# A second MLP product in seven block products for the latent tokens, its gate row formed on TensorE and its operand sums on GpSimd

## The chip, the cores and the metric

The kernel runs as one program on one core of a Trainium2 chip. The metric is device time of one execution in microseconds. TensorE (PE in the profile; PEld is its weight load) does the matrix products, VectorE (DVE) and ScalarE (ACT) the elementwise work, GpSimd (POOL) very little before the change, and SyncE (SP) issues nearly all DMAs.

## The reference, cut to what matters

One layer of a hybrid backbone over 640 tokens: 128 context tokens and 512 latent tokens, width 1024. The four mixers before the MLP are not touched by the change. What is touched is the end:

```python
shift1, scale1, gate1, shift2, scale2, gate2 = jnp.split(mod[:, None, :], 6, axis=-1)   # mod = silu(c) @ ada_w + ada_b
h2 = rmsnorm(x, norm2_g) * (1 + scale2) + shift2
ff = jnp.square(jax.nn.relu(h2 @ mlp_w1)) @ mlp_w2      # 640x1024 @ 1024x4096, then 640x4096 @ 4096x1024
x = x + gate2 * ff                                      # then one final rmsnorm
```

All of it is float32. Context rows use the gate of c_ctx, latent rows that of c.

## The kernel before, in words

**Precision.** Each float32 product is three passes in the type fp32r: an operand is split into a high part (a copy on ACT) and a low part (source minus high part, on DVE), and high x high, high x low and low x high are summed in PSUM. `split(hi, lo, src)` is this pair of instructions.

**The first MLP product** runs in 16 units of 256 columns of W1. A unit computes a 2x2 block product in seven block products (X11, X12, S2, S1, S3, S4, X22 of the weights with operands of the activations), each of 12 matmuls of 320 columns. The weight operands come from four raw blocks in WQ: sums of blocks on DVE (`sums`), then `split` into a ring XH/XL of 8 slots, made ahead of PE by up to 8 products. A unit holds a pair of PSUM banks A_ and B_. ACT copies a bank out and DVE adds the other (`rb<-ps,rb`, 128x320); then the bank is written on. So three DVE adds of a unit stand between products: the first half of r0 before S1 writes B_, the second half of r1 before X22 writes A_, the second half of r0 before the bank is used again. After them ACT applies Relu and Square to r0 and r1 (640 columns), and two splits store them as AH/AL (tiles olo).

**The second MLP product** is done per group of two units (8 groups, 512 rows of W2): four row blocks of W2 are loaded to w2raw and split into VH/VL (tiles vh, vl; 128x1024); for each of five token tiles, 4 x 3 passes x 2 halves = 24 matmuls of 512 columns, 120 in a group; DVE adds the result to ACC (tiles h), ten 128x512 adds in a group (ACT copies in the first group).

**gate2** is formed on DVE: the rows silu(c) are broadcast, and in groups 1 to 4 eight slices of ada_w are multiplied and summed along rows (`scalar_tensor_tensor` with an accumulator, 32 of 128x512). The finished row is broadcast after group 4.

**Order.** From the output projection on, all instructions are recorded and a planner (class Plan) emits them: PE keeps the recorded order; each other engine takes, among what its cost table holds to be ready, the instruction that is due first. Each engine then runs its list in that order. The table prices a GpSimd operation at 0.3 us plus n/450 us and a DVE one at 0.15 us plus n/960 us, each engine by itself. All these instructions have line 248 in the profile; they are told apart by tiles.

Of the kernel before, what the change touches and what calls it, by code (L numbers as in the profile page):

```python
# [7 lines left out]
F32 = mybir.dt.float32  # L8
# [400 lines left out]
def hybrid_step_kernel(ctx: ExitStack, tc: tile.TileContext, A: dict, O: dict):  # L409
# [860 lines left out]
    yhi["T2"], yhi["T3"], ylo["T2"], ylo["T3"] = pieces  # L1270
    AH, AL = oT["lo"][0:4], oT["lo"][4:8]
    PT = [tiles(psN, 2, [512], f"ps{i}_") for i in range(4)]

# [133 lines left out]

    NU, EARLY = 16, 4
    names = ("X11", "X12", "S2", "S1", "S3", "S4", "X22")
# [52 lines left out]

    rrot = [0]

    def next_r():
        rrot[0] = (rrot[0] + 1) % 3
        return RB[rrot[0]]

    def relu2(i, r):
        act.activation(r, r, AF.Relu)  # L1470
        act.activation(r, r, AF.Square)
        split(AH[i], AL[i], r)

    def unit(u, i):
        if u >= EARLY:
            first_products(u)
        A_, B_ = PT[ub[u]]
        a, b = A_[:, :HT], B_[:, :HT]
        r0, r1 = next_r(), next_r()
        act.activation(r0[:, :HT], a, AF.Copy)  # L1480
        dve.tensor_tensor(r0[:, :HT], b, r0[:, :HT], OP.add)
        product(u, "S2", "T2", A_, False)
        act.activation(r0[:, HT:], a, AF.Copy)
        product(u, "S1", "T1", B_, True)
        act.activation(r1[:, HT:], b, AF.Copy)
        product(u, "S3", "T3", A_, False)
        dve.tensor_tensor(r1[:, HT:], a, r1[:, HT:], OP.add)
        product(u, "S4", "Y22", B_, False)
        dve.tensor_tensor(r0[:, HT:], b, r0[:, HT:], OP.add)
        relu2(i, r0)  # L1490
        product(u, "X22", "T4", A_, False)
        act.activation(r1[:, :HT], a, AF.Copy)
        relu2(i + 1, r1)
        held.remove(ub[u])


    NG = 8
    half2 = lp.tile([128, 2, 8], F32, name="half2")

    def load_w2(g):  # L1500
        for i in range(4):
            raw = WRAW2[i % 2]
            nc.sync.dma_start(raw, A["w2"][2 * g + i // 2][:, D * (i % 2):D * (i % 2) + D])
            split(VH[i], VL[i], raw)

    def mm2(t, i, ps, halves=(0, 1)):
        ts_ = slice(128 * t, 128 * t + 128)
        for pi, (lh, rh) in enumerate(((AH, VH), (AH, VL), (AL, VH))):
            for n in halves:
                pe.matmul(ps[n], lh[i][:, ts_], rh[i][:, HALVES[n]], start=(i == 0 and pi == 0),  # L1510
                          stop=(i == 3 and pi == 2))

    def silu_rows():
        broadcast(flat(GATE), A["ccr"])
        jk = BIG[1][:, :512]
        for i in range(4):
            c = flat(GATE)[:, 512 * i:512 * i + 512]
            act.activation(jk, c, AF.Sigmoid)
            dve.tensor_tensor(c, c, jk, OP.mult)

    def gate2_part(i):
        wt, jk = BIG[0], BIG[1][:, :512]
        nc.sync.dma_start(wt, A["ada_g"][i])
        for cnd in range(2):
            for n in range(2):
                c = slice(512 * n, 512 * n + 512)
                dve.scalar_tensor_tensor(jk, wt[:, c], 1.0, GATE[:, cnd, c], op0=OP.mult, op1=OP.mult,
                                         accum_out=half2[:, n, cnd:cnd + 1])
            m = mod["gt2"][:, i, cnd:cnd + 1]
            dve.tensor_tensor(m, half2[:, 0, cnd:cnd + 1], half2[:, 1, cnd:cnd + 1], OP.add)  # L1530
            dve.tensor_tensor(m, m, P("adab", 40 + i), OP.add)

    fg = BIG[0]

    def finish_gate2():
        d = gate_rows("gt2", nc.sync)
        broadcast(flat(GATE), d)
        broadcast(fg, A["fg"])

    XA = []  # L1540

    def start_last():
        for t in range(NCH):
            XA.append(rp.tile([128, 4 * HT], F32, name=f"xa{t}", tag=("yh0", "yh1", "yl0", "yl1", "yh2")[t])[:, :D])
            nc.sync.dma_start(XA[t], x1d[t])
        for t in range(NCH):
            for n, c in enumerate(HALVES):
                a = ACC[n][:, t, :]
                dve.tensor_tensor(a, a, GATE[:, 0 if t == 0 else 1, c], OP.mult)
                dve.tensor_tensor(XA[t][:, c], XA[t][:, c], a, OP.add)  # L1550

    def last_tile(t, ps):
        x, y = XA[t], WRAW2[t % 2]
        for n, c in enumerate(HALVES):
            dve.tensor_tensor(y[:, c], ps[n], GATE[:, 0 if t == 0 else 1, c], OP.mult)
        dve.tensor_tensor(x, x, y, OP.add)
# [9 lines left out]
    def very_last(pairs):  # L1566
# [61 lines left out]
    first_products(2)  # L1628
    first_products(3)
    for g in range(NG):  # L1630
        last = g == NG - 1
        load_w2(g)
        for i in range(2):
            unit(2 * g + i, 2 * i)
        if last:
            start_last()
        pair = [PT[bank_pair()] for _ in range(2)]
# [4 lines left out]
        for t in range(NCH):  # L1642
            if last and t == NCH - 1:
# [6 lines left out]
            if last:  # L1650
                last_tile(t, ps)
                continue
            for n in range(2):
                a = ACC[n][:, t, :]
                if g == 0:
                    act.activation(a, ps[n], AF.Copy)
                else:
                    dve.tensor_tensor(a, ps[n], a, OP.add)
        if g == 0:
            silu_rows()  # L1660
        if 0 < g < 5:
            for i in range(2):
                gate2_part(2 * g - 2 + i)
        if g == 4:
            finish_gate2()
    with tc.manual_schedule():
# [3 lines left out]
def _arrays(inp):  # L1670
# [41 lines left out]
    for g, nm in enumerate(("rg_w_r", "rg_w_i")):  # L1712
# [50 lines left out]
```

## Time and profile before

| | |
|---|---|
| median of 3 runs | 820.03 us (819.25 to 823.0) |
| the profiled execution | 819.71 us, of which the span (first to last instruction) is 817.9 us |
| PE busy | 778.8 us, 95% |
| DVE busy | 575.2 us, 70% |
| ACT busy | 420.3 us, 51% |
| POOL busy | 23.4 us, 3% |

A busy PE tells only that a matmul is in the pipeline; how fast it goes is read from the starts of successive matmuls in the timeline. For the other engines busy time is occupancy. Durations of back-to-back DVE instructions overlap a little, so the distance of their starts is what one of them costs a full queue.

### The profile page before, as it was taken

What the parts mean: (1) busy time and instruction counts of PE and PEld (TensorE: products, weight loads), DVE (VectorE), ACT (ScalarE), POOL (GpSimd) and SP (SyncE); (2) the same over time, 40 slices, a digit from 0 to 9 for tenths busy, and PEclk for the clock granted to TensorE, in tenths of its full rate; (3) what the DMA queues carried; (4) which work ended last, traced back from release to release, by engine and by line L of the source; (5) the groups of instructions that cost most, each with busy time, mean ns of one, the idle gap of its engine ahead of it and who ended that gap; (6) DMA issues with size and microseconds to landing.
All of it is one profiled execution on the core that took longest, in us unless ns stands there. A gap on an engine that the chain in (4) does not pass through costs nothing.

```text
span 817.9 us, 13749 instructions
## 1 busy us (share of the span) xinstructions
PE 778.8 (95%) x5536; PEld 682.7 (83%) x5536; DVE 575.2 (70%) x1061; ACT 420.3 (51%) x708; POOL 23.4 (3%) x48
## 2 busy tenths in 40 slices
PE   4999999999999989999899999899999999999995
PEld 3798988768777889888888989789899898998984
DVE  4779988857786376368997888647466475675757
ACT  7533549688486332156784706417246172371533
POOL 0040000101010000000000000000000000000001
PEclk9999999999999999999999999999999999999998
DMA  9723323333321522543653636513132041330313
GB/s 352 304 83 137 105 95 142 116 110 100 125 84 56 104 103 65 194 155 127 204 165 102 195 97 204 119 40 117 50 131 75 20 136 52 101 106 2 128 52 128
DMA packets 33696, 97.79 MB, mean 120 GB/s; under 512 B 8672, under 2 KB 9696, under 8 KB 29024
## 3 DMA queue, kind: packets, MB, share of 16 engines
q1 hardware_dynamic: 32544, 95.72, 35.5%
q10 hardware_dynamic: 576, 1.00, 0.4%
q8 instruction: 43, 0.70, 0.3%
q0 software_dynamic: 512, 0.20, 0.1%
q14 instruction: 21, 0.17, 0.1%
HBM read 91.44 MB, written 5.46 MB: 118 GB/s over the span
## 4 chain that ended last, share of the span: by engine, by line
PE 63%; DVE 15%; ACT 10%; DMA 8%; issue 3%; SPq 0%; DVEq 0%; ACTq 0%
PE ps L248 45%; DMA wq<-in_w_dram 4%; ACT QbB L462 2%; DVE xl L248 2%; PE pjcx L492 2%; PE pjdb L492 2%; PE pja L666 2%; DMA w2raw<-in_wout_dram 1%; PE ap L536 1%; DVE wq L248 1%; DMA w2raw<-in_w_dram 1%; PE pjbqk L492 1%; DVE big L248 1%; PE rg L1132 1%; DMA rawdb<-in_win_dram 1%
## 5 line engine op out<-in xcount | busy, mean ns | idle before, releaser
L248 PE MATMUL ps<-vh,olo 128*128 128x512 f32 x680 | 186.4, 390 | 1.0 <-DVE olo L248 0.7
L248 PEld LDWEIGHTS ps<-vh,olo 128*128 128x128 f32 x680 | 126.9, 188 | 28.8 <-DVE olo L248 1.9
L248 PE MATMUL ps<-vl,olo 128*128 128x512 f32 x320 | 99.3, 390 | 0.0
L248 ACT ACTIVATE vh<-w2raw 128x1024 fp32r<-128x1024 f32 x32 | 33.8, 1057 | 118.6 <-PE ps L248 114.2
L248 ACT ACTIVATE xh<-wq 128x512 fp32r<-128x512 f32 x96 | 59.4, 628 | 61.1 <-PE ps L248 43.9
L248 PE MATMUL ps<-yh,xh 128*128 128x320 f32 x256 | 79.5, 311 | 1.2 <-DVE rb L248 1.2
L248 PE MATMUL ps<-yl,xh 128*128 128x320 f32 x256 | 79.0, 309 | 0.0
L248 PE MATMUL ps<-yh,xl 128*128 128x320 f32 x256 | 79.0, 308 | 0.0
L248 DVE TENSOR_TENSOR h<-ps,h 128x512 f32<-128x512 f32 x60 | 38.6, 686 | 52.9 <-PE ps L248 52.6
L248 PEld LDWEIGHTS ps<-vl,olo 128*128 128x128 f32 x320 | 60.1, 188 | 12.7
L248 DVE TENSOR_TENSOR xl<-wq,xh 128x512 fp32r<-128x512 f32 x96 | 64.8, 687 | 8.1 <-ACT xh L248 7.9
L248 PE MATMUL ps<-ohi,xh 128*128 128x320 f32 x256 | 57.1, 310 | 0.5 <-ACT xh L248 0.4
L248 ACT ACTIVATE rb<-rb 128x640 f32<-128x640 f32 x64 | 46.8, 734 | 7.6 <-DVE rb L248 6.8
L248 PEld LDWEIGHTS ps<-yh,xh 128*128 128x128 f32 x256 | 48.1, 188 | 2.0 <-DVE rb L248 1.5
L248 PEld LDWEIGHTS ps<-yl,xh 128*128 128x128 f32 x256 | 48.1, 188 | 0.3
L248 PEld LDWEIGHTS ps<-yh,xl 128*128 128x128 f32 x256 | 48.1, 188 | 0.0
L248 DVE TENSOR_TENSOR vl<-w2raw,vh 128x1024 fp32r<-128x1024 f32 x32 | 39.0, 1220 | 8.1 <-ACT vh L248 7.4
L248 PEld LDWEIGHTS ps<-ohi,xh 128*128 128x128 f32 x256 | 42.8, 188 | 1.1 <-ACT xh L248 0.6
L248 PE MATMUL ps<-ohi,xl 128*128 128x320 f32 x128 | 39.8, 311 | 0.5 <-DVE xl L248 0.4
L248 DVE TENSOR_TENSOR olo<-rb,olo 128x640 fp32r<-128x640 f32 x32 | 26.3, 821 | 18.6 <-ACT olo L248 18.6
L248 PE MATMUL ps<-t,xh 128*128 128x320 f32 x128 | 28.7, 311 | 0.7 <-DVE rb L248 0.7
L248 ACT ACTIVATE rb<-ps 128x320 f32<-128x320 f32 x64 | 27.1, 424 | 4.1 <-PE ps L248 4.1
(426 smaller groups left out, 1677.7 us busy)
## 6 DMA issues: line engine op xcount, KB each, us to landing
ar<-in_ada_w_dram SPq DMA_DIRECT2D x20, 1024.0 KB, 4.9
wq<-in_w_dram SPq DMA_DIRECT2D x72, 256.0 KB, 3.7
w2raw<-in_w_dram SPq DMA_DIRECT2D x32, 512.0 KB, 4.4
big<-in_ada_g_dram SPq DMA_DIRECT2D x8, 512.0 KB, 3.5
x<-in_x_dram SPq DMA_DIRECT2D x5, 512.0 KB, 6.8
big<-in_x_dram SPq DMA_DIRECT2D x5, 512.0 KB, 4.2
x1d<-big SPq DMA_DIRECT2D x5, 512.0 KB, 2.6
xa<-x1d SPq DMA_DIRECT2D x5, 512.0 KB, 4.5
```

The lines of the kernel that those rows point to most:

```text
L248: return fn(*[r(x) for x in a], **{w: r(v) for w, v in k.items()})
L462: act.activation(out, src, AF.Copy)
L492: pe.matmul(ps[:, n, :320], wt[:, k, c0:c0 + 128], h[:, k, s], start=(k == 0 and wt is hi and h is hhi), stop=stop)
L536: pe.matmul(ps[32 * g:32 * g + 32, :256], scx[:, 4 * j + g, 2 - 2 * vi:34 - 2 * vi], r3[:, 4 * j + g, :], start=(vi == 0 and j == 0), stop ...
L666: pe.matmul(d, w[:, k, 128 * j:128 * j + 128], (hlo if hi_ else hhi)[:, k, c], start=begin, stop=end, skip_group_check=(ch == "q" and i == 1))
L1132: pe.matmul(ps, wrg[:, dl, j, g, :], xc[:, hN * n:hN * n + hN], start=True, stop=True)
```

## The change

**Second product.** In groups 0 to 6, the four latent token tiles are taken as two halves of 256 tokens (columns 128 to 383 and 384 to 639 of r0, r1), the two row halves of the group as the inner halves, the two column halves of W2 as B11, B12, B21, B22. Seven block products replace eight, each of 2 token tiles x 2 x 3 = 12 matmuls of 512 columns. The context tile stays as it was, 24 matmuls. Group 7 keeps the old form.

**Operands.** For each unit, four sums of 256 columns on GpSimd and five splits in place of two. For each group, four weight sums of 1024 columns on GpSimd and eight splits of 128x1024 in place of four; VH and VL keep four slots, so T2, B12, T3 and T4 are split into slots that earlier products of the same stage leave free. The sum S1 of W1 blocks moves from DVE to GpSimd in all 16 units.

**Accumulation.** Each block product is added from its bank into one or two places of ACC: 16 adds in a group in place of ten.

**Storage.** The W1 ring goes from 8 slots to 6, and three units rather than four have their first products ahead of the groups. From group 0 on, the first products of the next group's first unit stand on PE in front of the second product.

**gate2.** The sixth slice of ada_w is multiplied on TensorE, in four quarters of 8 small matmuls and 2 transposes, in groups 1 to 4; the DVE products go. The broadcast of the finished row moves to group 6.

```diff
-    NU, EARLY = 16, 4
+    NU, EARLY = 16, 3
...
-        dve.tensor_tensor(S1, x21, x22, OP.add)
+        pool.tensor_tensor(S1, x21, x22, OP.add)
...
-        split(XH[q % 8], XL[q % 8], src)
+        split(XH[q % NX], XL[q % NX], src)          # NX = 6
...
+        split(QA[0][e], QA[1][e], r1)
+        lo, hi = slice(128, 384), slice(384, 640)
+        pool.tensor_tensor(A1, r0[:, hi], r1[:, hi], OP.add)
+        pool.tensor_tensor(r0[:, hi], r0[:, lo], r0[:, hi], OP.subtract)
+        split(operand("S1", 0, e), operand("S1", 1, e), A1)
+        pool.tensor_tensor(r0[:, lo], A1, r0[:, lo], OP.subtract)
+        pool.tensor_tensor(r1[:, lo], r1[:, lo], r0[:, lo], OP.subtract)
+        split(SA[0][e], SA[1][e], r0)
+        split(operand("S4", 0, e), operand("S4", 1, e), r1[:, lo])
...
+    def pieces_early():
+        r11, r12, r21, r22 = (RAW[n] for n in ("B11", "B12", "B21", "B22"))
+        piece("B11", 0, r11)
+        piece("B21", 1, r21)
+        pool.tensor_tensor(r11, r12, r11, OP.subtract)
+        piece("T1", 2, r11)
+        pool.tensor_tensor(r11, r22, r11, OP.subtract)
+        piece("B22", 3, r22)
+        pool.tensor_tensor(r22, r22, r12, OP.subtract)
+        pool.tensor_tensor(r21, r21, r11, OP.subtract)
...
+        both(0, "A11", "B11", True, [(0, 0)])
+        both(1, "A12", "B21", True, [(0, 0)])
+        ctx_part(0, "C1", "B11", True)
+        ctx_part(0, "C2", "B21", False)
+        accumulate(0, 0, ctxp[0])
+        piece("T2", 0, RAW["B11"])
+        piece("B12", 1, RAW["B12"])
+        both(1, "S1", "T1", True, [(1, 1)])
+        piece("T3", 2, RAW["B22"])
+        both(0, "S2", "T2", False, [(0, 1)])
+        both(1, "S4", "B22", False, [(0, 1)])
+        ctx_part(1, "C2", "B22", True)
+        piece("T4", 3, RAW["B21"])
+        both(0, "S3", "T3", False, [(1, 1)])
+        ctx_part(1, "C1", "B12", False)
+        accumulate(0, 1, ctxp[1])
+        for p in range(2):
+            product2(pairs[p][0], "A22", "T4", p, False)
...
+        for j in range(2):
+            for g in range(4):
+                pe.matmul(ps[32 * g:32 * g + 32, :256], scx[:, 4 * j + g, 2:34], BIG[j][:, 256 * g:256 * g + 256],
+                          start=(j == 0), stop=(j == 1))
```

**Where instructions stand: GpSimd.** Before, GpSimd's list holds nothing of the MLP but one multiplication in the last token tile (xa3 is that tile, big0 the final gain):

```order
L828 MEMSET du0_3411 128x8
L829 MEMSET du0_3411 128x8
L248 ISA
L248 TENSOR_TENSOR big1_3609<-xa3_7043,big0_3607 128x1024
L1759 UNCONDITIONAL_BRANCH
```

Now one middle group reads so (s1 is the W1 sum; big0, big1, w2raw0, w2raw1 are raw W2 blocks, so the 128x1024 rows are T1, T2, T3, T4; a1 and rb are sums of one unit):

```order
L248 TENSOR_TENSOR big0_3607<-big1_3609,big0_3607 128x1024
L248 TENSOR_TENSOR a1_4321<-rb1_4152,rb2_3909 128x256
L248 TENSOR_TENSOR rb1_4152<-rb1_4152 128x256
L248 TENSOR_TENSOR rb1_4152<-a1_4321,rb1_4152 128x256
L248 TENSOR_TENSOR rb2_3909<-rb2_3909,rb1_4152 128x256
L248 TENSOR_TENSOR s1_4061<-wq2_3563,wq3_3569 128x512
L248 TENSOR_TENSOR big0_3607<-w2raw1_3535,big0_3607 128x1024
L248 TENSOR_TENSOR w2raw1_3535<-w2raw1_3535,big1_3609 128x1024
L248 TENSOR_TENSOR w2raw0_3529<-w2raw0_3529,big0_3607 128x1024
L248 TENSOR_TENSOR a1_4321<-rb3_4100,rb0_4013 128x256
```

T1 stands in front of the first unit's sums, and T2, T3 and T4 directly behind the W1 sum, in front of the second unit's sums.

**Where instructions stand: VectorE.** Second unit of a middle group before, from the first r0 add (the row that reads a bank, ps) to the r1 add (the last row):

```order
L248 TENSOR_TENSOR rb1_4154<-ps1_1_3829,rb1_4154 128x320
L248 TENSOR_TENSOR xl6_3588<-wq0_3551,xh6_3586 128x512
L248 TENSOR_TENSOR olo5_3492<-rb0_4012,olo1_3488 128x640
L248 TENSOR_TENSOR xl7_3593<-wq1_3557,xh7_3591 128x512
L248 TENSOR_TENSOR wq0_3551<-s1_4140,wq0_3551 128x512
L248 TENSOR_TENSOR xl1_3561<-s1_4140,xh1_3559 128x512
L248 TENSOR_TENSOR wq1_3557<-wq1_3557,wq0_3551 128x512
L248 TENSOR_TENSOR xl0_3555<-wq0_3551,xh0_3553 128x512
L248 TENSOR_TENSOR xl2_3567<-wq2_3563,xh2_3565 128x512
L248 TENSOR_TENSOR rb2_3909<-ps1_0_3826,rb2_3909 128x320
```

The same stretch now:

```order
L248 TENSOR_TENSOR rb3_4100<-ps0_1_3623,rb3_4100 128x320
L248 TENSOR_TENSOR sg_4334<-a1_4321,sg_4334 128x256
L248 TENSOR_TENSOR xl4_3578<-wq0_3551,xh4_3576 128x512
L248 TENSOR_TENSOR olo2_3489<-rb2_3909,olo0_3487 128x640
L248 TENSOR_TENSOR vl2_3544<-big0_3607,vh2_3542 128x1024
L248 TENSOR_TENSOR xl5_3583<-wq1_3557,xh5_3581 128x512
L248 TENSOR_TENSOR olo6_3493<-rb1_4152,olo4_3491 128x640
L248 TENSOR_TENSOR sg_4334<-rb2_3909,sg_4334 128x256
L248 TENSOR_TENSOR wq2_3563<-wq0_3551,wq2_3563 128x512
L248 TENSOR_TENSOR rb0_4013<-ps0_0_3621,rb0_4013 128x320
```

Between the two bank adds there are now splits of the first unit's operands (sg, olo) and of T1 (vl2), and one W1 sum (wq2) that needs GpSimd's s1.

## Rows read from the trace of the kernel before

**Rows 1.** The page: busy time, share of the span and instructions.

```profile
PE 778.8 (95%) x5536; PEld 682.7 (83%) x5536; DVE 575.2 (70%) x1061; ACT 420.3 (51%) x708; POOL 23.4 (3%) x48
```

**Rows 2.** Busy time in stretches: the first group, another; then stages of one group.

```profile
core 0: us, PE busy (x) PEld busy (x) DVE busy (x) ACT busy (x) POOL busy (x), PEclk, DMA share, GB/s
391.00:442.00 51.00, 47.65 (x266) 42.15 (x266) 47.34 (x86) 35.66 (x64) 0.00 (x0) 1.00 0.51 163
546.00:598.00 52.00, 52.00 (x290) 47.13 (x289) 30.77 (x46) 22.87 (x39) 0.00 (x0) 1.00 0.26 81
...
574.20:601.40 27.20, 27.20 (x122) 22.52 (x121) 11.66 (x16) 6.29 (x9) 0.00 (x0) 1.00 0.09 30
601.40:613.70 12.30, 12.30 (x86) 12.26 (x85) 9.55 (x14) 7.43 (x13) 0.00 (x0) 1.00 0.66 217
613.70:626.10 12.40, 12.40 (x86) 12.40 (x86) 9.68 (x16) 9.41 (x18) 0.00 (x0) 1.00 0.24 65
```

**Rows 3.** PE's timeline: matmuls of 320 and of 512 columns, one group's second product to the next's.

```profile
471.86 0.62 PE L248 MATMUL ps<-vl,olo 128*128 128x512 f32 x2
...
473.22 0.62 PE L248 MATMUL ps<-vl,olo 128*128 128x512 f32 x2
...
496.58 0.31 PE L248 MATMUL ps<-yh,xl 128*128 128x320 f32 x1
...
497.02 0.31 PE L248 MATMUL ps<-yh,xl 128*128 128x320 f32 x1
...
574.27 0.63 PE L248 MATMUL ps<-vh,olo 128*128 128x512 f32 x2
...
626.13 0.62 PE L248 MATMUL ps<-vh,olo 128*128 128x512 f32 x2
```

**Rows 4.** Groups of instructions by shape: busy, mean ns | idle before.

```profile
L248 DVE TENSOR_TENSOR xl<-wq,xh 128x512 fp32r<-128x512 f32 x96 | 64.8, 687 | 8.1 <-ACT xh L248 7.9
L248 DVE TENSOR_TENSOR vl<-w2raw,vh 128x1024 fp32r<-128x1024 f32 x32 | 39.0, 1220 | 8.1 <-ACT vh L248 7.4
L248 DVE TENSOR_TENSOR olo<-rb,olo 128x640 fp32r<-128x640 f32 x32 | 26.3, 821 | 18.6 <-ACT olo L248 18.6
L536 PE MATMUL ap<-ar,scx 128*32 128x256 f32 x320 | 22.0, 383 | 1.9 <-DMA ar<-in_ada_w_dram 1.4 <-ACT o2a L1073 0.5
L248 PE MATMUL ps<-con,w2raw 128*128 128x128 f32 x8 | 1.1, 280 | 1.8 <-DVE w2raw L248 1.8
L527 POOL MEMSET scx<- 128x272 f32 x1 | 0.3, 324 | 0.0
```

**Rows 5.** DVE's timeline: a 256-column instruction; then the second unit of a group.

```profile
372.05 0.42 DVE L248 TENSOR_TENSOR yl<-h,yh 128x256 fp32r<-128x256 f32 x1
...
616.87 0.69 DVE L248 TENSOR_TENSOR s<-wq,wq 128x512 f32<-128x512 f32 x1 [0.76 <-DMA wq<-in_w_dram]
...
618.20 0.48 DVE L248 TENSOR_TENSOR rb<-ps,rb 128x320 f32<-128x320 f32 x1
618.60 0.68 DVE L248 TENSOR_TENSOR xl<-wq,xh 128x512 fp32r<-128x512 f32 x1
619.20 0.82 DVE L248 TENSOR_TENSOR olo<-rb,olo 128x640 fp32r<-128x640 f32 x1
619.93 0.68 DVE L248 TENSOR_TENSOR xl<-wq,xh 128x512 fp32r<-128x512 f32 x1
...
623.55 0.48 DVE L248 TENSOR_TENSOR rb<-ps,rb 128x320 f32<-128x320 f32 x1
```

**Rows 6.** PE's timeline in the same unit: product X22 (tile t) begins.

```profile
624.37 0.45 PE L248 MATMUL ps<-t,xh 128*128 128x320 f32 x2
```

**Rows 7.** PE's waits from 390 us on: total, times, longest.

```profile
PE ps L248 <- DVE rb L248: 1.9, 3, 1.2
```

**Rows 8.** Timeline of GpSimd and DVE in the last token tiles.

```profile
806.57 2.41 POOL L248 TENSOR_TENSOR big<-xa,big 128x1024 f32<-128x1024 f32 x1 [496.33 <-DMA out_y_dram<-xa]
806.69 0.69 DVE L248 TENSOR_TENSOR w2raw<-ps,gate 128x512 f32<-128x512 f32 x1 [0.35 <-PE ps L248]
...
807.41 2.11 DVE L248 TENSOR_TENSOR xa<-xa,w2raw 128x512 f32<-128x512 f32 x1
...
811.58 0.68 DVE L248 TENSOR_TENSOR xa<-xa,w2raw 128x512 f32<-128x512 f32 x1
```

More of the change, by code (lines that the diff above doesn't have):

```diff
@@ L1461, in first_products, with relu2, operand, unit @@
             product(u, ("X11", "X12")[i], ("Y11", "Y21")[i], PT[ub[u]][i], True)
-    rrot = [0]
+    rrot, side = [0], []
     def next_r():
-        rrot[0] = (rrot[0] + 1) % 3
+        rrot[0] = (rrot[0] + 1) % 4
         return RB[rrot[0]]
[L1469 to L1475, printed above, removed]
+    def relu2(r, c):
+        act.activation(r[:, c], r[:, c], AF.Relu)
+        act.activation(r[:, c], r[:, c], AF.Square)
+    sg = {}
+    def operand(op, part, e):
+        if op == "A11":
+            return PA[part][:, 256 * e:256 * e + 256]
+        t = SA if op in ("C1", "S2", "S3") else QA
+        if op in ("C1", "C2"):
+            return t[part][e][:, :128]
+        if op in ("A12", "A22", "S2", "S3"):
+            o = 128 if op in ("A12", "S2") else 384
+            return t[part][e][:, o:o + 256]
+        o = 0 if op == "S1" else 256
+        return sg["t"][:, part, e, o:o + 256]
+    def unit(u, e, seven):
+        if u not in ub:
             first_products(u)
@@ L1497, in hybrid_step_kernel @@
+        pool.tensor_tensor(r1[:, lo], r1[:, lo], r0[:, lo], OP.subtract)
+        split(SA[0][e], SA[1][e], r0)
+        split(operand("S4", 0, e), operand("S4", 1, e), r1[:, lo])
     NG = 8
[L1498 removed]
+    RAW = {"B11": BIG[0], "B12": BIG[1], "B21": WRAW2[0], "B22": WRAW2[1]}
+    V = {}
     def load_w2(g):
[L1501 to L1504, printed above, removed]
+        for i, n in enumerate(("B11", "B21", "B12", "B22")):
+            nc.sync.dma_start(RAW[n], A["w2"][g, {"B11": 0, "B12": 1, "B21": 2, "B22": 3}[n]])
@@ new lines, in product2, with accumulate @@
+    def product2(bank, op, n, p, start):
+        for e in range(2):
+            ops = [operand(op, part, e)[:, 128 * p:128 * p + 128] for part in range(2)]
+            for i, (l, r) in enumerate(((0, 0), (0, 1), (1, 0))):
+                pe.matmul(bank, ops[l], V[n][r][:, 512 * e:512 * e + 512], start=(start and e == 0 and i == 0),
+                          stop=(e == 1 and i == 2), skip_group_check=True)
+    begun = set()
+    def accumulate(t, n, ps):
+        a = ACC[n][:, t, :]
+        if (t, n) not in begun:
+            begun.add((t, n))
+            act.activation(a, ps, AF.Copy)
+        else:
+            dve.tensor_tensor(a, ps, a, OP.add)
@@ L1506, in mm2 @@
     def mm2(t, i, ps, halves=(0, 1)):
         ts_ = slice(128 * t, 128 * t + 128)
-        for pi, (lh, rh) in enumerate(((AH, VH), (AH, VL), (AL, VH))):
+        e, h = i // 2, i % 2
+        for l, r in ((0, 0), (0, 1), (1, 0)):
             for n in halves:
[L1510 to L1531, printed above, removed]
+                w = V[(("B11", "B12"), ("B21", "B22"))[h][n]][r][:, 512 * e:512 * e + 512]
@@ L1533, in hybrid_step_kernel @@
     fg = BIG[0]
+    gate2 = {}
     def finish_gate2():
-        d = gate_rows("gt2", nc.sync)
-        broadcast(flat(GATE), d)
-        broadcast(fg, A["fg"])
+        gate2["t"] = rp.tile([128, 2, D], F32, name="gate2", tag="gate")
+        broadcast(flat(gate2["t"]), gate2["rows"])
     XA = []
@@ L1628, in hybrid_step_kernel @@
     first_products(2)
-    first_products(3)
     for g in range(NG):
         last = g == NG - 1
-        load_w2(g)
+        if g == 0:
+            sg["t"] = rp.tile([128, 2, 2, 512], F32R, name="sg", tag="gate")
         for i in range(2):
-            unit(2 * g + i, 2 * i)
-        if last:
-            start_last()
+            unit(2 * g + i, i, not last)
+            if i == 0:
+                load_w2(g)
+                if last:
+                    for j, n in enumerate(("B11", "B21", "B12", "B22")):
+                        piece(n, j, RAW[n])
+                    broadcast(fg, A["fg"])
+                else:
+                    pieces_early()
+        if not last:
+            if 2 * g + 2 not in ub:
+                first_products(2 * g + 2)
+            seven_products(g)
+            if g < 4:
+                side.append(gate2_quarter(g))
+                next(side[0])
+            if g == 4:
+                gate2["rows"] = gate_rows("gt2", nc.sync)
+            if g == NG - 2:
+                finish_gate2()
+            continue
+        start_last()
         pair = [PT[bank_pair()] for _ in range(2)]
@@ L1649, in hybrid_step_kernel @@
                     mm2(t, i, ps)
[L1650 to L1665, printed above, removed]
+            last_tile(t, ps)
     with tc.manual_schedule():
```

76 lines of the change are left out of this document (61 added, 15 removed).

## The prediction, made before the changed kernel was run

> **What bounds the kernel now.** I read the page's busy shares first, then busy time by stretches, PE's and DVE's timelines inside one group, PE's waits, and last the one place where GpSimd and VectorE work at once. PE is busy for 778.8 of 817.9 us [rows 1], and in a middle group for all of 52.00 us [rows 2]. Starts of matmuls show that it is also at its pace: six matmuls of 512 columns take 473.22 - 471.86 = 1.36 us, 0.227 each, and three of 320 columns 0.44 us, 0.147 each, each with its own weight load [rows 3]. A group lasts from one second product to the next, 626.13 - 574.27 = 51.86 us: 120 x 0.227 = 27.2 and 14 products x 12 x 0.147 = 24.7. From 390 us on PE waited for the bank adds on DVE 1.9 us in all [rows 7]. So the MLP is bound by PE, with DVE at 30.8 of 52 us [rows 2].
>
> That average hides where DVE is tight. In the 27.2 us of the second product it is busy for 11.66; in the units for 9.55 of 12.30 and 9.68 of 12.40 [rows 2]. In the second unit it runs without a break from 618.20, and the r1 add ends at 623.55 + 0.48 = 624.03 [rows 5], while X22, which must wait for it, begins at 624.37 [rows 6]. The margin is 0.3 us. In front of that add DVE has no slack even now.
>
> **PE's part.** Seven of eight block products: 12 matmuls of 512 columns fewer in each of 7 groups, 84 x 0.227 = 19.0 us off the bounding engine. gate2 adds 32 small matmuls and 8 transposes: 22.0 / 320 = 0.069 each gives 2.2 us, and 1.1 us for eight 128x128 ones [rows 4], together +3.3. The DVE products of gate2 that go stood beside a busy PE and give nothing back by themselves. Sum for PE: -15.7 us; a group then takes 49.1 us plus waits.
>
> **DVE's part.** One instruction costs a full queue its duration less about 0.08 us: 0.60 for 512 columns, 0.73 for 640, 0.40 for a bank add [rows 5], and so 1.14 for 1024 [rows 4] and 0.34 for 256 [rows 5]. A group now has 14 weight splits (8.4), 6 sums (3.6), 6 bank adds (2.4), six splits of 256 and four of 640 (5.0), eight of 1024 (9.1) and 16 adds to ACC (9.6): 38.1 us, against 29.2 before by the same count. Alone, 38.1 would fit into 49.1. ACT has about 23 us in a group [rows 2] and gains four 1024-column copies and some small ones, some 7 us; it stays clear.
>
> The stretch in front of the r1 add of the second unit, by the order now: two sg (0.7), two xl (1.2), two olo (1.5), T1's split (1.1), one W1 sum (0.6), the add (0.4), 5.5 us. Before it was 624.03 - 618.60 = 5.4 us. So the margin of 0.3 us stays what it was, unless something is added there.
>
> **GpSimd's part.** Something is. A group has four operations of 1024 columns, two of 512 and eight of 256. The trace has one such operation, 2.41 us for 1024 [rows 8]. The smaller ones are bounded by 2.41 above and by a GpSimd fill of 272 columns, 0.32 us, below [rows 4]. I take 0.1 us plus a share by columns, 1.25 and 0.68, since the fill shows that size counts: 9.6 + 2.5 + 5.4 = 17.6 us in a group. The Trainium skill (GPSIMD Engine Reference, section 3.1) gives 4497 ns for an add of 2048 columns; with the 2.41 us that would be an estimate of 1.36 and 0.84, or 19.1 us in a group. No run here shows it yet.
>
> What GpSimd does to DVE stands in rows 8. While GpSimd multiplied two SBUF tiles (806.57 to 808.98), a DVE operation with PSUM as one source took its usual 0.69 us. The next, with both sources in SBUF, took 2.11 us where the same form took 0.68 later, and ended 0.54 us after GpSimd did: it did not share, it stood still to the end. A stopped DVE instruction saves only 0.14 us of its own, so a 1024-column sum costs a DVE queue that is full of splits about 2.2 us, one of 512 columns 1.1. Splits and sums have both sources in SBUF (26 of DVE's 38.1 us); bank and ACC adds (12.0 us) do not. The Trainium skill (SBUF — State Buffer, section Who interferes with whom) says the same of both forms, and adds that whichever starts first holds the pair for its whole instruction, so that GpSimd would wait for DVE too. The trace agrees as to DVE (2.11 against 0.68); it shows nothing of the other side. By that rule the two would take turns, which is the upper end below, and the sum 846.
>
> **Where it lands.** In groups 1 to 4 GpSimd's order has the W1 sum of 512 columns, then T2, T3 and T4 of 1024 each, one behind the other. The W1 sum can start when its blocks have landed, about 616.9 in the old frame, where DVE waited 0.76 us for that transfer [rows 5]; T2 needs T1's split, which comes at about the same place. That is in front of the r1 add. Behind it stand PE's X22 and all that follows in its fixed order; the ring of six ready weight operands doesn't help, as the wait is for a bank. If only the W1 sum and T2 get in before the add: 1.1 + 2.2 - 0.3 = 3.0 us of PE waiting in the group. If DVE and GpSimd alternate, all four do: 7.4. A case between (T3 in, T4 behind) is 5.2, and I take that: 4 x 5.2 = 20.8 us. T1 in the first unit I cost at nothing: DVE has 12.30 - 9.55 = 2.7 us free there, and with that cover gone it would be 2.2 a group.
>
> In group 0 DVE is busy for 47.34 of 51.0 us and PE already idles 3.3 [rows 2], so there is no cover at all: between two 1024-column operations (4.4) and three quarters of all GpSimd time (13); I take 8. In groups 5 and 6 no gate slice occupies the raw buffers, and T1 to T4 stand ahead of the first unit's sums; only a W1 sum remains before the add, 0.8 each, up to 3.3 with one 1024-column operation; I take 2, so 4. Waits: 20.8 + 8 + 4 = 33 us, between 18 and 49.
>
> Left at nothing: the shorter ring and the three early units (the order of PE's work is the same; without cover about one operand split, 0.7 us, per unit); slots of VH reused within the stage (T4 has the two products S3 and C1, 4.1 us, for a copy and a split of 2.3 us and two handovers); the later broadcast of gate2 (a whole unit phase lies between); PE's clock, which stood at 1.00, the upper level, even where PE idled 3.3 of 51 us [rows 2].
>
> **Sum.** -19.0 + 3.3 + 33 = +17.3 us on the profiled execution's 819.71 gives 837.0; the median is 0.3 above that execution, so 837. The likeliest case's own range is +2.3 to +33.3, 822 to 853.
>
> **Rivals.** *GpSimd finds the gaps: faster.* At 49.1 us a group, DVE has 11.0 us idle and 12.0 us of adds from PSUM, 23 us of room for 17.6. For it: adds from PSUM are not stopped [rows 8], and sixteen adds lie in the second product. Against it: the sums stand in the units, not there. It holds where T2 to T4 run behind the r1 add; then at most 1 us a group is lost, and the time is 820 - 15.7 = 804 to 811. Chance 0.22.
>
> *DVE's queue mostly goes first: no change.* GpSimd gets in only when DVE pauses; one wait of about 2.2 us a group remains, 7 x 2.2 = 15.4, which eats the gain: 820. For it: DVE's list is dense there. Against it: DVE itself waits for the W1 sum, which lets GpSimd in. Chance 0.13.
>
> *GpSimd becomes a bound of its own: slower still.* The second unit's four sums stand behind T2 to T4; if these are held up to the end of the unit, the split for the context tile comes late in the second product, and 2 to 3 us a group are added to the upper end: 850 to 865. Chance 0.10, part of slower.
>
> That leaves 0.55 for the forecast, 0.65 for slower in all. 0.5%, 4 us, is about what a measurement can tell from no change. The range of 8 in 10 is 806 to 856: it takes in most of the faster case, where some wait is likely, and stops short of the worst.
>
> **What would show it.** Right: DVE splits of 512 columns with durations of 1.5 to 3 us where a GpSimd operation of 1024 columns ends; a PE wait for DVE rb of 3 to 7 us at X22 of the second unit in groups 1 to 4; ACC adds at their old 0.69; second products of 24.5 us without a gap. Wrong: GpSimd's sums inside the second product, PE waits under 1 us a group, a group of 49 to 50 us; or PE waiting for a vh or vl split in the second product, which would put the loss on the slots.

## The result and the profile after

The changed kernel takes 873.04 us (median of 4, 868.88 to 874.74) where the kernel before takes 821.51 on the same chip: a ratio of 1.062 [1.057, 1.067], 51.5 us slower. The forecast was 837, with a range up to 856: the side was right, and so was the way in which GpSimd stops VectorE; the size was not. The profiled execution has a span of 871.5 us.

The page answers to [rows 1]: PE is busy for 9.7 us more than before, though it does fewer matmuls, DVE for 110, POOL for 161.

```profile
PE 788.5 (90%) x5524; PEld 688.9 (79%) x5524; DVE 685.4 (79%) x1065; ACT 457.0 (52%) x792; POOL 184.0 (21%) x148
```

The groups by shape (busy, mean ns | idle before) answer to [rows 4]. The 512-column split, 687 ns before, now has a mean of 902; a 1024-column sum on GpSimd takes 2.77 us against 2.41 [rows 8]; the bank add, which has PSUM as one source, stays at 0.48 [rows 5].

```profile
L248 DVE TENSOR_TENSOR xl<-wq,xh 128x512 fp32r<-128x512 f32 x96 | 85.5, 902 | 16.5 <-ACT xh L248 16.4
L248 POOL TENSOR_TENSOR w2raw<-w2raw,big 128x1024 f32<-128x1024 f32 x14 | 38.6, 2770 | 2.7 <-DVE vl L248 2.4
L248 POOL TENSOR_TENSOR s<-wq,wq 128x512 f32<-128x512 f32 x16 | 25.1, 1568 | 122.3 <-DMA wq<-in_w_dram 122.3
L248 DVE TENSOR_TENSOR rb<-ps,rb 128x320 f32<-128x320 f32 x48 | 23.0, 480 | 2.5 <-PE ps L248 2.5
```

The timeline of the second unit of group 1 (start, duration, instruction, idle before) answers to [rows 5, 6] and shows where the loss arises.

```profile
483.00 1.73 POOL L248 TENSOR_TENSOR s<-wq,wq 128x512 f32<-128x512 f32 x1
483.51 1.90 DVE L248 TENSOR_TENSOR olo<-rb,olo 128x640 fp32r<-128x640 f32 x1
484.69 2.93 POOL L248 TENSOR_TENSOR big<-w2raw,big 128x1024 f32<-128x1024 f32 x1
485.33 2.57 DVE L248 TENSOR_TENSOR sg<-rb,sg 128x256 fp32r<-128x256 f32 x1
485.52 0.31 PE L248 MATMUL ps<-yh,xl 128*128 128x320 f32 x1
487.69 5.18 POOL L248 TENSOR_TENSOR w2raw<-w2raw,big 128x1024 f32<-128x1024 f32 x2
487.82 2.82 DVE L248 TENSOR_TENSOR wq<-wq,wq 128x512 f32<-128x512 f32 x1
490.57 0.48 DVE L248 TENSOR_TENSOR rb<-ps,rb 128x320 f32<-128x320 f32 x1
490.97 2.45 DVE L248 TENSOR_TENSOR wq<-s,wq 128x512 f32<-128x512 f32 x1
491.10 0.91 PE L248 MATMUL ps<-t,xh 128*128 128x320 f32 x2 [5.27 <-DVE rb L248]
...
494.47 0.47 PE L248 MATMUL ps<-yh,xh 128*128 128x320 f32 x1
494.74 0.47 PE L248 MATMUL ps<-yl,xh 128*128 128x320 f32 x1
...
497.02 0.30 PE L248 MATMUL ps<-yl,xh 128*128 128x320 f32 x1
497.16 0.31 PE L248 MATMUL ps<-yh,xl 128*128 128x320 f32 x1
...
499.07 0.40 PE L248 MATMUL ps<-vh,xh 128*128 128x512 f32 x1
```

Read it as a zip. A GpSimd sum ends at 484.73, 487.62, about 490.3; the DVE instruction that was stopped ends 0.3 to 0.7 us behind it, and while it ends, the next sum already stands. One DVE instruction passes for each sum, in 1.9 to 2.8 us where the same forms took 0.42 to 0.82 [rows 5]. The product in front of the bank add is done at 485.52 + 0.31 = 485.83, but the add stands in DVE's queue behind two stopped instructions and starts at 490.57. From the start of the W1 sum (483.00) to the add, three instructions with two SBUF sources stand in the queue (olo, sg, wq), so three sums get in: the W1 sum, T2 and T3. T4 starts at about 490.3, just before the add, and stops the instruction behind it (490.97, 2.45 us). PE waits 5.27 us for the add, and then runs slow: 320-column matmuls start 0.27 us apart, against 0.147 [rows 3], until 496.87; the next second product begins at 499.07. PE's waits for that add, 1.9 us in all before [rows 7]:

```profile
PE ps L248 <- DVE rb L248: 26.2, 6, 6.0
```

The other five of these waits are in groups 2 to 6. In groups 2 to 4 GpSimd's and VectorE's instructions come in the same order as in group 1, with T4 again too late for the add. In groups 5 and 6 it is X22 of the first unit, not of the second, that waits: there T3 and T4 run on GpSimd from 706.67 to 712.72 and from 760.88 to 766.93 us, and VectorE is stopped in front of the first unit's add.

```profile
550.97 0.90 PE L248 MATMUL ps<-t,xh 128*128 128x320 f32 x2 [6.02 <-DVE rb L248]
609.68 0.90 PE L248 MATMUL ps<-t,xh 128*128 128x320 f32 x2 [5.83 <-DVE rb L248]
671.54 0.90 PE L248 MATMUL ps<-t,xh 128*128 128x320 f32 x2 [3.77 <-DVE rb L248]
714.33 0.56 PE L248 MATMUL ps<-t,xh 128*128 128x320 f32 x2 [2.66 <-DVE rb L248]
768.53 0.56 PE L248 MATMUL ps<-t,xh 128*128 128x320 f32 x2 [2.66 <-DVE rb L248]
```

The stretches answer to [rows 2]: first the group 0 stage and another group's, then group 0's second product, one of the usual ones and the units behind it, and the five microseconds around that wait (PE, PEld, DVE, ACT, POOL busy, granted clock, DMA share, GB/s).

```profile
391.00:442.00 51.00, 33.42 (x182) 30.27 (x181) 46.05 (x62) 29.69 (x61) 27.98 (x15) 0.84 0.27 83
546.00:598.00 52.00, 47.03 (x256) 41.72 (x257) 44.87 (x57) 25.18 (x45) 17.95 (x12) 0.93 0.31 94
...
422.90:464.30 41.40, 28.69 (x110) 22.16 (x109) 32.31 (x32) 20.52 (x36) 19.47 (x13) 0.84 0.25 77
...
499.07:523.90 24.83, 24.83 (x111) 20.31 (x110) 20.41 (x28) 7.03 (x10) 2.10 (x3) 1.00 0.32 103
523.90:558.10 34.20, 28.18 (x187) 27.00 (x186) 31.38 (x34) 21.47 (x43) 19.04 (x11) 0.90 0.22 70
490.00:495.00 5.00, 3.90 (x14) 3.90 (x15) 5.00 (x7) 2.49 (x5) 2.87 (x2) 0.50 0.00 0
```

From group 1 on a second product runs without a gap (24.83 us); all the loss is in the units, and in group 0, whose product takes 41.4. From 490 to 495 the granted clock is 0.50, the lower level (1.2 GHz), after 5.27 us without a matmul. One more wait was in nobody's list. In group 4 PE stands for 3.82 us until 664.31, in the middle of the second unit; the chain of waits there (start, duration, what) runs over a W1 load that takes 8.05 us, issued behind the store of gate2's rows.

```profile
654.60 8.05 DMA wq<-in_w_dram
662.65 0.02 issue
662.68 0.64 ACT xh L248
```

### The profile page after: what moved, and what is told of

It is laid out like the page before. It is cut to its first block, busy times and chain, and to the rows that moved or that the text cites. A ratio compares the mean times of both kernels' runs of the same rounds, so it can differ in the third digit from the quotient of the medians.

```text
span 871.5 us, 14039 instructions
## 1 busy us (share of the span) xinstructions
PE 788.5 (90%) x5524; PEld 688.9 (79%) x5524; DVE 685.4 (79%) x1065; ACT 457.0 (52%) x792; POOL 184.0 (21%) x148
## 4 chain that ended last, share of the span: by engine, by line
PE 54%; DVE 23%; ACT 10%; DMA 6%; issue 5%; POOL 1%; SPq 0%; DVEq 0%; ACTq 0%; POOLq 0%
PE ps L248 39%; DVE xl L248 4%; DMA wq<-in_w_dram 2%; ACT QbB L462 2%; DVE wq L248 2%; DVE sg L248 2%; PE pjdb L492 2%; PE pjcx L492 2%; PE pja L666 2%; DVE vl L248 1%; DMA w2raw<-in_wout_dram 1%; DVE olo L248 1%; PE ap L536 1%; DVE rb L248 1%; PE pjag L492 1%
## 5 line engine op out<-in xcount | busy, mean ns | idle before, releaser
L248 PE MATMUL ps<-vh,olo 128*128 128x512 f32 x456 | 142.6, 392 | 1.2 <-DVE olo L248 1.2
L248 PEld LDWEIGHTS ps<-vh,olo 128*128 128x128 f32 x456 | 86.2, 189 | 20.1 <-DVE olo L248 1.6
L248 DVE TENSOR_TENSOR xl<-wq,xh 128x512 fp32r<-128x512 f32 x96 | 85.5, 902 | 16.5 <-ACT xh L248 16.4
L248 PE MATMUL ps<-vl,olo 128*128 128x512 f32 x208 | 79.0, 392 | 0.0
L248 DVE TENSOR_TENSOR h<-ps,h 128x512 f32<-128x512 f32 x102 | 67.1, 682 | 11.5 <-PE ps L248 11.5
L248 ACT ACTIVATE rb<-rb 128x320 f32<-128x320 f32 (+1 forms) x80 | 45.5, 572 | 39.8 <-DVE rb L248 38.7
L248 PE MATMUL ps<-t,xh 128*128 128x320 f32 x128 | 35.3, 367 | 26.4 <-DVE rb L248 26.2
L248 PEld LDWEIGHTS ps<-yh,xh 128*128 128x128 f32 x256 | 51.5, 201 | 6.5 <-ACT rb L248 4.6
L248 ACT ACTIVATE vh<-big 128x1024 fp32r<-128x1024 f32 x30 | 31.8, 1059 | 45.8 <-PE ps L248 37.2
L248 PEld LDWEIGHTS ps<-yl,xh 128*128 128x128 f32 x256 | 51.2, 200 | 0.0
L248 POOL TENSOR_TENSOR s<-wq,wq 128x512 f32<-128x512 f32 x16 | 25.1, 1568 | 122.3 <-DMA wq<-in_w_dram 122.3
L248 POOL TENSOR_TENSOR big<-big,big 128x1024 f32<-128x1024 f32 x7 | 21.8, 3121 | 133.7 <-DVE vl L248 133.7
L248 PEld LDWEIGHTS ps<-t,xh 128*128 128x128 f32 x128 | 25.6, 227 | 29.0 <-DVE rb L248 29.0
```

Of the source, the lines that this page charges most:

```text
L248: return fn(*[r(x) for x in a], **{w: r(v) for w, v in k.items()})
```

## The experiments

The first question was whether the two engines' turn-taking carries the loss, or the denser operand work by itself; the second, what the other parts cost. Each ratio is to the kernel before on the same chip.

**All sums on VectorE.** Every `pool.tensor_tensor` that the change put on GpSimd goes to DVE:

```diff
-        pool.tensor_tensor(S1, x21, x22, OP.add)
+        dve.tensor_tensor(S1, x21, x22, OP.add)
...
-        pool.tensor_tensor(r11, r12, r11, OP.subtract)
+        dve.tensor_tensor(r11, r12, r11, OP.subtract)
```

> All operand sums (the W1 sum, the four unit sums, T1 to T4) are back on VectorE, everything else as in the changed kernel. Theory (a running GpSimd sum stops every VectorE instruction with both sources in SBUF): GpSimd is out of the MLP, VectorE has 38.1 + 8.5 = 46.6 us of work in a group of about 50, so PE waits under 2 us a group: 808 to 825 us, and splits of 512 columns are at 0.69 us. Rival (VectorE is simply overfull by the change): another 8.5 us of work in each of seven groups makes it slower than the changed kernel, 880 us or more.

Measured: 820.52 us, ratio 0.998 [0.995, 1.001]. 100 more instructions on the denser engine are 52.5 us faster than the same sums on the idle one (873.04 - 820.52). DVE is then busy for 47 to 48 us of a group of 49.4 to 51.4, and PE for nearly all of it. So the denser operand work by itself is not the loss. One group stands out, group 4 from 578.2 to 636.6:

```profile
526.80:578.20 51.40, 51.32 (x297) 45.52 (x296) 47.41 (x77) 28.94 (x52) 0.00 (x0) 1.00 0.31 103
578.20:636.60 58.40, 52.81 (x295) 46.97 (x295) 47.93 (x78) 29.15 (x52) 0.00 (x0) 0.97 0.33 91
686.00:735.40 49.40, 49.40 (x278) 44.88 (x277) 48.21 (x77) 29.29 (x52) 0.00 (x0) 1.00 0.29 92
```

**Only T1 to T4 on VectorE, and only T1 to T4 on GpSimd.** The same edit for the four T sums of a group alone, and for the ten others alone.

> Only T1 to T4 (the 1024-column sums) go to VectorE; the W1 sum and the unit sums stay on GpSimd, 8 us a group. Theory: the long stops go, short ones of 0.5 to 1.2 us stay: 810 to 830 us. Rival (overfull VectorE): 4.6 us more work a group, 875 us or more.

> The other half: the W1 sum and the unit sums go to VectorE, T1 to T4 stay on GpSimd. Theory: T2 to T4 still stop VectorE before its bank add in the second unit in most groups: 840 to 868 us, with stretched splits beside the 1024-column sums. Rival (overfull VectorE): 4 us more work a group, 880 us or more. Rival (what hurts is the length of GpSimd's own queue): 8 us less queue, about as e2.

Measured: 835.56 us, 1.016 [1.011, 1.021], and 858.78, 1.045 [1.040, 1.050]. So the T sums cost 37.5 us (873.04 - 835.56), or 38.3 counted from the other side (858.78 - 820.52), and the W1 and unit sums 15.0 or 14.3: the parts add up. The first came out 5.6 us above its range: PE still waits 1.4 to 1.7 us at X22 in each of groups 1 to 3, and 4.72 us in group 4 for a W1 load, of which more below.

**Fills in place of the sums.** Each GpSimd sum, and the product in the last token tiles, becomes two fills of its output; what they compute is left out.

```diff
+            if eng == "POOL" and op == "tensor_tensor" and self.size(out) in (256, 512, 1024) and self.fill:
+                for _ in range(2):
+                    self.nc.gpsimd.memset(r(out), 0.5)
+                return None
```

> Each GpSimd sum (and the one product in the last token tiles) is replaced by two fills of the same tile at the same place of GpSimd's list, so that GpSimd writes and stays busy about as long but reads nothing; the sums are left out. Theory (it is GpSimd's reading that stops VectorE): VectorE's splits return to 0.69 us and the time falls to 806 to 822 us. Rival (overfull VectorE, or GpSimd's queue comes late): VectorE's work and GpSimd's order are the same, so 860 to 875 us.

Measured: 816.90 us, 0.993 [0.990, 0.995]. GpSimd is busy for 101 us more than before (161 in the changed kernel), its results are waited for in the same places, and DVE's split is back at 684 ns:

```profile
L253 DVE TENSOR_TENSOR xl<-wq,xh 128x512 fp32r<-128x512 f32 x96 | 64.9, 684 | 22.8 <-ACT xh L253 22.4
```

Thus neither GpSimd's slowness nor a handover of its results is the loss; that GpSimd reads is. The Trainium skill (SBUF — State Buffer, section Who interferes with whom) says that a DVE instruction with two SBUF inputs contends with a GpSimd instruction that reads SBUF, not with one that only writes it; this pair of runs agrees (902 ns with reads, 684 without).

**T1 to T4 not formed.** The four lines are left out, so T1 to T4 hold raw blocks; the W1 and unit sums stay on GpSimd.

> T1 to T4 are not formed at all (their splits take the raw blocks, so the second product is not the reference's); the rest is as in the changed kernel. Theory: without the 1024-column sums the waits of PE in the second unit go, 806 to 822 us. Rival (overfull VectorE): its work is unchanged, 860 us or more.

Measured: 829.19 us, 1.007 [1.004, 1.010]. Out of its range by 7: with 512 and 256 columns alone 12.3 us are left over the run of fills, about the 15.0 of above. PE's wait at X22 in groups 1 to 3 is down to 0.2 us, as the theory said; a wait of 4.85 us in group 4 is the one for the W1 load again.

**Four idle sums in the kernel before.** Nothing of the change, only four unused 1024-column sums on GpSimd in the first unit of each of groups 5 and 6:

```diff
+        if u in (10, 12):
+            for j in range(4):
+                pool.tensor_tensor(BIG[1], VH[3].bitcast(F32), BIG[0], OP.add)
         product(u, "S4", "Y22", B_, False)
```

> The kernel before, with eight GpSimd additions of two 1024-column SBUF tiles whose result nobody uses, four each in groups 5 and 6. Theory: VectorE's splits beside them take 1.5 to 3 us, and as VectorE has 21 us free in a group PE waits 0 to 4 us in each: 821 to 830 us. Rival (no stopping): splits stay at 0.69 us, 821 us.

Measured: 838.12 us, 1.017 [1.013, 1.022]: 15.1 us for eight sums that nobody reads, 1.9 each, about twice the most expected. In the timeline the zip is alone:

```profile
661.50 11.47 POOL L248 TENSOR_TENSOR big<-vh,big 128x1024 f32<-128x1024 f32 x4 [351.74 <-ACT vh L248]
661.78 3.44 DVE L248 TENSOR_TENSOR vl<-w2raw,vh 128x1024 fp32r<-128x1024 f32 x1
665.14 2.87 DVE L248 TENSOR_TENSOR xl<-s,xh 128x512 fp32r<-128x512 f32 x1
667.94 2.82 DVE L248 TENSOR_TENSOR xl<-wq,xh 128x512 fp32r<-128x512 f32 x1
670.68 0.48 DVE L248 TENSOR_TENSOR rb<-ps,rb 128x320 f32<-128x320 f32 x1
...
671.22 0.90 PE L248 MATMUL ps<-t,xh 128*128 128x320 f32 x2 [4.67 <-DVE rb L248]
```

Four sums in a row take 11.47 us, 2.87 each against 2.41 alone [rows 8]: GpSimd waits for DVE too. PE waits 4.67 us in group 5 and 6.83 in group 6, and for 4 us behind each wait the granted clock is 0.50: from this X22 to the next one PE takes 14.29 and 14.57 us, where it took 12.31 before. So these waits cost 2.0 and 2.3 us more than they last.

**Filler matmuls in PE's wait.** In groups 1 to 4, 32 matmuls into a spare bank stand in front of X22 of the second unit, so that PE doesn't idle there.

```diff
+    NFILL = 32
...
+        if seven and e == 1 and 0 < u // 2 < 5:
+            spare = PT[next(x for x in last_used if x not in held)][0]
+            for j in range(NFILL):
+                pe.matmul(spare[:, :HT], yhi["Y11"][:, j % 4, :128], yhi["Y22"][:, j % 4, :], start=True, stop=True,
+                          skip_group_check=True)
```

> The changed kernel with 32 extra matmuls of 320 columns into an idle bank just before X22 of the second unit in groups 1 to 4, where PE waits 3.8 to 6 us; they are 4.7 us of work at full clock. Theory on the clock (the wait itself lets the granted clock fall to half, and the products after it then run at 0.267 instead of 0.147 us): PE stays busy, the clock stays at 1.00 there, and 2 to 4 us a group come back: 857 to 868 us although PE does 19 us more. Rival (the lower clock has another cause): 873 us or more.

Measured: 874.74 us, 1.063 [1.057, 1.069]; the changed kernel's own time. The granted clock stayed at 1.00 in the units of groups 1 to 3, and they got shorter (in group 2, 32.45 us against 34.20), but each second product behind them got longer (26.64 against 24.83). Group 2 kept its 59.1 us, and at the end of group 3's product, 641.04 us against 641.32, nothing is left of the gain. In group 4 the clock fell all the same (0.91 over its units), behind the wait for the W1 load, and the 32 matmuls took 5.7 us there. In group 2:

```profile
496.36:523.00 26.64, 25.61 (x110) 20.05 (x109) 21.55 (x30) 9.78 (x15) 4.00 (x5) 1.00 0.39 119
523.00:555.45 32.45, 31.01 (x219) 29.95 (x218) 30.29 (x32) 19.66 (x37) 17.89 (x10) 1.00 0.22 66
```

So in groups 1 to 3 the slow clock is not a second loss that could be had back by itself: what PE gained in the units it lost in the next product, where it waited 0.86 us for a W2 split on DVE. This run and the first together suggest that VectorE's lateness sets the group's 59 us; which of its handovers takes the rest of the product's 1.8 us was not followed up.

**The old second product in all groups**, with the rest of the change (W1 sums on GpSimd, gate2 on PE, the shorter ring).

> All eight groups use the old second product; everything else is as changed: W1 sum on GpSimd, gate2 on TensorE, ring of 6, three early units, two storage tiles less. Theory: 821 us plus 4.6 us of gate2 on PE plus little for one W1 sum of GpSimd per unit, where VectorE has room: 823 to 835 us. Rival (ring, early units or gate2 carry the loss): 850 us or more.

Measured: 839.82 us, 1.020 [1.014, 1.026], above its range. Its largest idle stretch is one wait of 7.04 us in group 4; a wait of 3.8 to 7.0 us stands there in every run so far that has the new gate2. It follows the store of gate2's rows (4-byte pieces from 128 partitions into DRAM): the W1 load behind it lands late. In the run with all sums on VectorE that is the chain of waits at 616 us:

```profile
616.29 0.11 DVE xl L248
616.40 8.69 DMA wq<-in_w_dram
...
626.18 13.86 PE ps L248 x74
```

**The store on another queue, in four parts, and later.** Three runs with all sums on VectorE, and one of the changed kernel:

```diff
-                gate2["rows"] = gate_rows("gt2", nc.sync)
+                gate2["rows"] = gate_rows("gt2", nc.scalar)
```

> All sums on VectorE, and the store of gate2's rows (two DMAs of 4 KB, from SBUF into DRAM) issued on ScalarE's queue instead of SyncE's; nothing else changes. In e1_all_dve PE waited 5.2 us once, in group 4, for a W1 block whose load stood on SyncE's queue right behind these two stores, and a landing there took 8.5 to 10 us. Theory: the loads wait for their turn in SyncE's queue behind the stores. Then the wait of 5.2 us and the dip behind it go, group 4 falls from 58.4 to 51 to 52 us, and the time is 812 to 815. Rival 1: the stores hold up the DMA engines themselves, whichever queue they come from; then the wait stays at 4 to 5 us and the time at 818 to 822. Rival 2: the wait has another cause, the W1 buffer comes free late; then the time is 818 to 822 as well, and the wait stays in the run with the store in quarters too.

> All sums on VectorE, and gate2's rows stored in four parts, each behind its own quarter (eight DMAs of 1 KB on SyncE's queue, two in each of groups 1 to 4) instead of two DMAs of 4 KB. Theory (the size of the store sets how long the W1 load behind it waits): each pair now holds a W1 load up by about a quarter of 10 us, 2.5, which the loads' lead covers; the wait of 5.2 us goes, time 812 to 816. Rival 1 (the stores take DMA engines, from any queue): the same here, 812 to 816, so that this run and the one with ScalarE's queue together tell the two apart. Rival 2 (the wait isn't from the stores): a PE wait of 4 to 5 us stays in group 4, 818 to 822.

> The changed kernel with its sums on GpSimd as they are, and only gate2's rows stored in four parts behind their quarters. Theory: of the changed kernel's loss the store makes the wait of 3.8 us at 664 us and some of the slow clock behind it, so 4 to 8 us go: 865 to 869, ratio 1.052 to 1.058. Rival (the DVE backlog is what paces that group as well, and covers the wait): within 2 us of the changed kernel, 871 to 875.

Measured: on ScalarE's queue 822.68 us, 1.001 [0.999, 1.004]; in four parts 837.46, 1.018 [1.014, 1.022]; the changed kernel in four parts 879.05, 1.070 [1.067, 1.073]. All three theories failed, and the last two times lie outside every range that was given for them. The queue is not the cause: the load behind still takes 10.53 us, and PE waits 7.04 for it. Nor does a smaller store help: behind two stores of 1 KB a load takes 7.08, and four pairs of stores give four waits (4.16, 4.91, 2.58 and 3.59 us). The chain of waits, first of ScalarE's queue, then of four parts:

```profile
616.84 10.53 DMA wq<-in_w_dram
```

```profile
634.10 7.08 DMA wq<-in_w_dram
```

The Trainium skill (DMA: Bandwidth & Descriptors, section Issuing engines are not separate DMA queues) says that DMAs of any issuing engine run on the same 16 DMA engines; the first of these runs agrees. Why a quarter of the bytes still holds a load up is left open. The kernel before has the same two stores, at 507.38 and 509.69 us of its trace, and PE waits 1.19 us there once; so the store itself is not new. What remains is the place; here the store is ordered behind the context tile's second sum of group 4:

```diff
+                plan.late = {ctx_done[0]}
                 gate2["rows"] = gate_rows("gt2", nc.sync)
+                plan.late = set()
```

> All sums on VectorE, and the store of gate2's rows (two DMAs of 4 KB on SyncE's queue, as in the change) ordered behind the second half of the context tile's sum in group 4, so that it stands behind the last W2 load of group 5 and in front of the W1 loads of group 6, which in e1_all_dve began some 11 us later. Theory, by the runs with ScalarE's queue and with quarters (a W1 load that follows the store closely lands in 7 to 10 us instead of 3.4, from either queue and for a quarter of the bytes): where no load follows for 10 us the store holds up nothing, the wait of 5 to 7 us in group 4 goes, the group falls from 58 to 51 to 52 us, and the time is 812 to 816, ratio 0.988 to 0.994. Rival (the wait of group 4 is of the gate's part on TensorE in that unit, or of the W1 buffers, not of the store): a wait of 4 to 7 us stays in group 4, 819 to 823. Second rival: the store holds up the W2 block in front of it or the W1 loads behind it in group 5, and the wait is only moved there: 818 to 823.

Measured: 812.49 us, 0.988 [0.984, 0.992], faster than the kernel before and than the change. The store now stands 11 us ahead of the next W1 load (651.05 and 662.25 us); the slowest W1 load lands in 7.0 us, and group 4 takes 51.2 where it took 58.4, which is 7.2 of the 8.0 us between the two runs:

```profile
526.10:577.90 51.80, 51.41 (x297) 45.51 (x296) 47.34 (x77) 28.74 (x52) 0.00 (x0) 1.00 0.32 102
577.90:629.10 51.20, 51.06 (x297) 45.47 (x295) 47.62 (x78) 29.19 (x53) 0.00 (x0) 1.00 0.32 103
679.00:728.40 49.40, 49.40 (x279) 44.92 (x278) 48.45 (x78) 29.63 (x53) 0.00 (x0) 1.00 0.29 93
```

```profile
DMA to landing us min/median/max: 2.9/3.4/7.0
```

The changed kernel itself, with its sums on GpSimd, was not run with the store in this place.

## Why the prediction was wrong

The last run has the change's PE work, no sums on GpSimd and no wait for the store, so the changed kernel against it, stretch by stretch, is the prediction's term "waits", and the run itself is its term "PE":

| term | predicted us | measured us (how) |
|---|---|---|
| PE, -19.0 + 3.3 | -15.7 | -9.6 (812.49 against 822.12) |
| groups 1 to 4, the wait at X22 | 20.8 (5.2 each; 3.0 to 7.4) | 20.9 (5.27, 6.02, 5.83 and 3.77) |
| groups 5 and 6, the same | 4 (2 each) | 5.3 (2.66 each, in the first unit) |
| groups 1 to 6, PE's matmuls behind these waits | 0 | 12.8 (2.7, 1.9, 1.6, 2.9, 1.9 and 1.9) |
| group 0, GpSimd | 8 (4.4 to 13) | 16.0 |
| store of gate2's rows | 0 | 3.8 (the wait in group 4; with all sums on VectorE the store cost 7.2) |

The stretches go from one second product's start to the next, for group 0 to its product's end and for group 1 from there. These points are at 464.35, 499.07, 558.11, 616.51, 679.71, 733.91 and 788.13 us in the changed kernel's timeline and at 448.31, 474.35, 526.11, 577.89, 629.10, 678.99 and 728.37 in the last run's. So group 1 lost (499.07 - 464.35) - (474.35 - 448.31) = 8.7 us, and groups 1 to 6 lost 8.7, 7.3, 6.6, 12.0, 4.3 and 4.8, 43.7 in all; the terms of the table leave 0.9 of them open. With group 0 it is 788.13 - 728.37 = 59.8 us, as the spans have it: 871.5 - 812.0 = 59.5. What stands behind a wait is measured from X22 to the next second product, in groups 5 and 6 to the next X22. In group 1 it is 499.07 - 491.10 = 7.97 us, and in the last run 5.28:

```profile
469.07 0.45 PE L249 MATMUL ps<-t,xh 128*128 128x320 f32 x2
...
474.35 0.40 PE L249 MATMUL ps<-vh,xh 128*128 128x512 f32 x1
```

- **What bounds it, the margin of 0.3 us, and the wait at X22 in groups 1 to 4** were right: PE waits in the second unit, for the bank add, and 20.9 us of it came where 20.8 were forecast. That DVE stands still to the end of a sum was right (902 ns, the timeline). That adds from PSUM aren't stopped was right, at 0.48 us. The case that was taken, T3 in and T4 behind, is the one that came in all four groups. But no row had spoken for it, and it came by the rule that was held to give 7.4: the engines do alternate strictly, and only three instructions that can be stopped are left in front of the add. So that it fitted is partly luck.
- **The step that failed is to take the wait in front of one add for the whole loss of a group.** Groups 1 to 6 lost 43.7 us where 24.8 were forecast, and only 26.2 of them are waits for a bank add. Behind each of these waits PE's matmuls start 0.27 us apart, and it comes to the next second product (or X22) 1.6 to 2.9 us later than in the last run, 12.8 us in all. The prediction had left PE's clock at nothing, because it stood at 1.00 where PE idled 3.3 of 51 us [rows 2]; the waits here, 2.66 to 6.02 us in one piece, were each followed by the lower level. The clock is not alone in it: in the run with fillers it stayed at 1.00 in groups 1 to 3 and the same time went one product later, so VectorE, which T4 stops once more behind the add, is late there as well (0.86 us of wait for a W2 split).
- **Groups 5 and 6**: "only a W1 sum remains before the add" looked at the second unit. The wait came in the first, where T3 and T4 stop VectorE in front of that unit's add.
- **Group 0** was bounded by "three quarters of all GpSimd time (13)" and took 16.0. In its second product PE waits 5.76, 5.77 and 1.18 us for splits of operands, and the granted clock was 0.84 there. How much of the 16.0 is clock was not tried.
- **gate2**: its row's store was not in the list of terms at all. In the changed kernel PE waits 3.8 us for the load behind it; what a later store would give there was not shown.
- **PE's gain** came out at 9.6 of 15.7. gate2 takes 1.00 us for a quarter's matmuls and 0.13 for its transposes (4.5 in all, not 3.3), and a group with every sum on DVE takes 49.4 to 51.8 us where 49.1, or 49.9 with gate2, were worked out. A second product takes 24.8 us even where PE doesn't wait in it, not 24.5, and in two of them PE waits 0.64 and 0.39 us for an ACC add. The rest was not followed up.

Against the forecast of +17.3 us the terms come to 33 more: 18.9 in groups 1 to 6, 8.0 in group 0 and 6.1 in PE's gain. With every wait at its upper end (49) the sum would still have been 853.

The rivals: GpSimd doesn't find the gaps. "DVE's queue mostly goes first" doesn't hold either. "GpSimd becomes a bound of its own" gave a time nearer to the measured one (850 to 865), but by a mechanism that didn't come: no second product of groups 1 to 6 has a gap.

## What to carry to other kernels

Before a step is moved to an idle GpSimd, ask what the engine beside it reads: if VectorE's queue is dense with instructions of two SBUF operands, each GpSimd sum that reads costs it about its whole duration, and the sum is cheaper in VectorE's own queue. Where two engines take turns, count the instructions that can be stopped in front of the handover: that many sums get in, here three. Then don't take the wait at the handover for the whole loss, but ask what runs behind it, on PE at a lower clock and on VectorE still late. And list the DMAs of a moved step with what is queued behind them in the new place: two stores of 4 KB in 4-byte pieces cost 7.2 us in front of a load that is needed soon, more than the 4.5 us of PE's work for the whole step.

## What the runs showed that was not expected

- Eight sums on GpSimd that nobody uses cost 15.1 us in a kernel whose VectorE is busy for 59% of a group [rows 2].
- A W1 load takes 3.4 us to land (the median of the last run; 7.0 at most), and 7.1 to 10.5 in the waits shown here behind a row store, from either queue, with two stores of 4 KB or of 1 KB.
- A slow clock behind PE's waits need not cost anything of its own: taking it away in three groups left the time where it was (874.74 against 873.04). With VectorE free, in the run with idle sums, it came with 2.0 and 2.3 us on top of the waits.
